# Two-layer decoder trunk on one core: when the MLP's turned hidden features are rounded, and five buffers for raw weight chunks instead of four

## The chip, the cores and the metric

One core of one Trainium2 chip runs the whole trunk in one launch. The metric is the device time of one execution in microseconds. The kernel before has a median of 2459.55 us in three runs (2457.21 to 2461.0).

## What is computed

Batch 1, 256 tokens, width 2048, two layers, all in float32. The part that the change concerns is the MLP of each layer, which has 8192 hidden features:

```python
for i in range(DEPTH):                      # DEPTH = 2
    hn = rmsnorm(h, attn_norm_g[i])
    ...                                     # attention, mixer A or B
    hn = rmsnorm(h, mlp_norm_g[i])
    h = h + jnp.square(jax.nn.relu(hn @ mlp_w1[i])) @ mlp_w2[i]
    gate = jax.nn.sigmoid(rmsnorm(h, ple_norm_g[i]) @ ple_w_gate[i])
    h = h + (p[i] @ ple_w_proj[i]) * gate
return rmsnorm(h, final_norm_g)
```

## The kernel before

**Split products.** Every float32 product is made of three products of rounded numbers. A weight chunk is a tile of 128 x 1024 (512 KB). `load` (L230) brings it from HBM into a `raw` buffer, issued by SP; `copy` (L242) rounds it to `whi` on ScalarE (ACT); `sub` (L250) makes `wlo` = `raw` - `whi` on VectorE (DVE). TensorE (PE) then multiplies `whi` with the high and the low part of the other operand, and `wlo` with the high part. There are 4 buffers `raw`, 6 `whi` and 5 `wlo`.

**The order of the work.** `Program.run` writes one static order. For each chunk, in the order in which PE uses them, it first issues loads as far ahead as the `raw` buffers go (a load waits until the buffer's last reader is done), then the rounding and the subtraction of the chunk some four and three places ahead, then lets every running generator go one `yield` further, then issues PE's matmuls of the chunk. So one `yield` is one chunk of PE's work, and an engine takes its instructions strictly in the order in which they were written: an ACT instruction that waits for a transfer holds up every later `whi`.

**The MLP** (`mlp`). The hidden features are cut into 4 blocks b of 2048, a block into 4 groups q of 512. An "up" gives 256 tokens x 512 features (tokens on partitions); a "down" needs the features on partitions. Groups 0 and 1 of block 0 are made by `ups`, all others two at a time by `up_mixed`, which takes 22 chunk steps: ten of 12 matmuls and three times four steps a, b, t, u of 6, 3, 6 and 6, for which DVE also adds weights (L530 makes `ts`, L535 and L536 change `raw` in place). `downs_pair` follows: 16 chunk steps of 12 matmuls. The order is: ups(0; 0, 1), up_mixed(0; 2, 3), then for each block b: downs_pair(b; 0, 1), up_mixed(b+1; 0, 1), downs_pair(b; 2, 3), up_mixed(b+1; 2, 3). The first downs_pair of a block uses group 2 from its ninth step on and group 3 from its thirteenth.

**How a group is turned** (`up`, called by `up_plain` and by `done` in `up_mixed`; `turned` and `bounce` below it). ACT scales and clips (L798) and squares (L755); DVE transposes 32 x 32 squares into the tile `z` (L699); POOL writes `z` to HBM (`dU`, L196) and, when that has landed, reads it back in another arrangement with four transfers (L200) into `w`, `t` or `y`; ACT rounds the result into the high part of `h` (L763), DVE subtracts for the low part (L765), and PE's downs read `h`. How many `yield`s stand between these steps decides where each is in its engine's order. Before, there are two between square and transpose (for the second group of a mixed pair four: `late` = 2), and one between the end of `turned` and the rounding.

**Elsewhere.** `sum_halves`, `to_head`, `key_unit`, `q_done` and `proj_done` use two small tiles of pool `E`: `es` (written by ACT at L389, read by DVE at L391) and `rsh` (written and read by DVE).

Of the kernel before, what the change touches and what calls it, by code (L numbers as in the profile page):

```python
# [10 lines left out]
F32 = mybir.dt.float32  # L11
# [4 lines left out]
P = 128  # L16
D = 2048
T = 256
# [15 lines left out]
UNIT_AHEAD = (0, 1, 2, 4, 5)  # L34
DMA_AHEAD = 7
SPLIT_AHEAD = 3
RAW_BUFS, HI_BUFS, LO_BUFS = 4, 6, 5
MIXED = (2, 3, 5)

G_ATTN, G_MLP, G_PLE, G_KV, G_FIN = 0, 2, 4, 6, 7  # L40
# [2 lines left out]
def f32(ap):  # L43
    return ap.bitcast(F32)
# [116 lines left out]
def kernel(ctx: ExitStack, tc: tile.TileContext, a: dict, out: bass.AP):  # L161
# [13 lines left out]
    cur = {}  # L175
# [6 lines left out]
    def close_pool(key):  # L182
        cur.pop(key)
        cur.pop(key + "/es").close()
# [200 lines left out]
                nc.tensor.matmul(ps[:, :T], lo[:, col:col + P], rhs[:, :T], start=False, stop=last)  # L385

    def sum_halves(ps):
        s = cur["E"].tile([P, T], F32, tag="es", name="es", bufs=4)
        nc.scalar.copy(s, ps[:, :T])  # L389
        t = cur["E"].tile([P, T], F32, tag="et", name="et", bufs=7)  # L390
        nc.vector.tensor_add(t, ps[:, T:], s)  # L391
        return t
# [203 lines left out]
    def to_head(ps, norm, dst, roped, mark, late=0, lo=None):  # L596

        t = sum_halves(ps)
        for _ in range(1 + late):
            yield  # L600
        while norm.r is None:
            yield
        if callable(dst):
            dst = dst()
        elif dst is None:
            dst = t
        if not roped:
            nc.vector.tensor_mul(dst, t, norm.rb)
        else:
            sh = cur["E"].tile([32, T], F32, tag="rsh", name="rsh", bufs=2)  # L610
            nc.vector.stream_shuffle(sh, t[:32, :], ROPE_SWAP)
            nc.vector.tensor_mul(dst, t, norm.rc)
            nc.vector.tensor_mul(sh, sh, norm.rs)
            nc.vector.tensor_add(dst[:32, :], dst[:32, :], sh)
        if lo is not None:
            yield
            nc.scalar.copy(lo[0], dst)
            yield
            nc.vector.tensor_sub(lo[1], dst, f32(lo[0]))
        mark()  # L620
# [107 lines left out]
    def mlp(layer, xg, norm, to, norm2, opening):  # L728

        y = [None] * 4
        hid = [[None] * 16 for _ in range(NFB)]
        forms = [None] * (KT // 2)

        def new(n):
            return cur["h"].tile([P, D // 2], F32, tag=n, name=n, bufs=1)  # L740

        def row():
            return cur["z"].tile([P, 2, 512], F32, tag="t", name="t", bufs=2)

        def second(n):

            return flat(row()) if n == "z" and hid[-1][-1] else flat(row_tile())

        def other(n):

            return flat(row()) if n == "w" else new(n)

        def up(b, q, t, late=0):

            nc.scalar.activation(t, t, AF.Square)  # L755
            for _ in range(2 + late):
                yield
            w = yield from turned(t, second if b == 0 and q == 1 else other if q % 2 else new, nc.gpsimd)
            yield
            w4 = w.rearrange("p a (i j r) -> p a (i j) r", j=2, r=32)  # L760
            h = cur["z"].tile([P, 2, 4, T], F32R, tag="h", name="h", bufs=4)
            h5 = h.rearrange("p c i (j a r) -> p c a (i j) r", j=2, r=32)
            nc.scalar.copy(h5[:, 0], w4)  # L763
            yield
            nc.vector.tensor_sub(h5[:, 1], w4, f32(h5[:, 0]))  # L765
            for i in range(4):
                hid[b][4 * q + i] = (h[:, 0, i], h[:, 1, i])

        def up_plain(b, q, ps0, ps1, mm):

            while norm.col is None:
                yield
            t = row()
            for j, ps in enumerate((ps0, ps1)):
                nc.scalar.activation(t[:, j], ps, AF.Relu, scale=norm.col[:, j:j + 1])
            yield from up(b, q, t)

        def up_mixed(b, q):

            ts = []  # L780

            def sums(aux):
                s, o = row(), row()
                nc.scalar.copy(s[:, 0], aux["P1"])
                yield
                nc.vector.tensor_sub(s[:, 1], aux["R6"], s[:, 0])
                nc.vector.tensor_add(o[:, 0], aux["Q5"], s[:, 1])
                nc.vector.tensor_sub(s[:, 1], aux["Q7"], s[:, 1])
                nc.vector.tensor_sub(o[:, 1], o[:, 0], aux["Q7"])
                ts.extend((s, o))  # L790

            def done(i, ps):
                while not ts:
                    yield
                t = ts[i]
                nc.vector.tensor_add(t, ps, t)
                for j in range(2):
                    nc.scalar.activation(t[:, j], t[:, j], AF.Relu, scale=norm.col[:, j:j + 1])  # L798
                yield from up(b, q + i, t, 2 * i)

            c0, c1, c2, c3, c4 = [c for c in range(KT // 2) if c not in MIXED]
            m0, m1, m2 = [(c,) for c in MIXED]
            order = [(0, c0), (0, c1), m0, (0, c2), (1, c0), m1, (0, c3), (1, c1), m2, (0, c4), (1, c2), (1, c3), (1, c4)]
            pair_major(lambda i, c: a["w1"][layer * 128 + (b * 4 + q + i) * 8 + c], order, xg, forms, sums, done)

        def normed(k):
            return renorm(k, G_PLE + layer, to, norm2)

        def down(b, q, ps0, ps1, mm):
            if b == 0:  # L810
                y[q] = row_tile()
            for j, ps in enumerate((ps0, ps1)):
                if b:
                    nc.vector.tensor_add(y[q][:, j], ps, y[q][:, j])
                else:
                    nc.scalar.copy(y[q][:, j], ps)
            if b < NFB - 1:
                return
            yield
            w = yield from turned(y[q], second if q == 1 else new)  # L820
            add_turned(q, w)
            yield
            yield from in_pairs(normed, q)

        def chunks(w, b, q):
            return lambda c: a[w][layer * 128 + (b * 4 + q) * 8 + c]

        def ups(b, q, hooks=None):
            token_major(chunks("w1", b, q), xg, lambda *ps: up_plain(b, q, *ps), hooks, whole=True)

        def downs(b, q):
            token_major(chunks("w2", b, q), hid[b], lambda *ps: down(b, q, *ps), whole=True)

        def all_forms():
            for c in MIXED:
                yield from x_forms(2 * c, G_MLP + layer, forms)
                yield
        taken_late(lambda: ups(0, 0, {4: [lambda: norm.factor(rows=True)]}), lambda: ups(0, 1), opening,
                   [all_forms])
        def downs_pair(b, q):  # L840
            taken_late(lambda: downs(b, q), lambda: downs(b, q + 1))

        up_mixed(0, 2)
        for b in range(NFB):
            downs_pair(b, 0)
            if b < NFB - 1:
                up_mixed(b + 1, 0)
                downs_pair(b, 2)
                up_mixed(b + 1, 2)
        downs(NFB - 1, 2)  # L850
        downs(NFB - 1, 3)
        prog.op(lambda: close_pool("z"))
        prog.op(lambda: open_pool("j"))

    def flat(t):
        return t.rearrange("p j c -> p (j c)")

    def row_tile():

        return cur["h"].tile([P, 2, 512], F32, tag="y", name="y", bufs=4)  # L860
# [14 lines left out]
    def ple(layer, pg, xg, norm, nxt, norm2, last):  # L875
# [182 lines left out]

        for q in range(4):
            def proj_done(f, ps, q=q):  # L1060
                s = cur["E"].tile([P, T], F32, tag="es", name="es", bufs=4)
                nc.scalar.copy(s, ps[:, :T])
                t = cur["j"].tile([P, T], F32, tag="pj", name="pj", bufs=8)
                nc.vector.tensor_add(t, ps[:, T:], s)
                pj[4 * q + f] = t
                return
                yield
# [321 lines left out]
    def key_unit(n, i, which, at, hooks=None):  # L1389

        def done(ps0, ps1, mm):
# [3 lines left out]
            for g in range(GB):  # L1395
# [2 lines left out]
                k4, c4, s4 = (v.rearrange("p (j a r) -> p j a r", j=2, a=4) for v in  # L1398
                              (cur["E"].tile([P, T], F32, tag="et", name="et", bufs=7), n_b1.rc, n_b1.rs))
                src = w.rearrange("p a (g j r) -> p g j a r", j=2, r=32)[:, g]  # L1400
                sh = cur["E"].tile([32, T], F32, tag="rsh", name="rsh", bufs=2)
                sh4 = sh.rearrange("p (j a r) -> p j a r", j=2, a=4)
                nc.vector.tensor_mul(k4, src, c4)
                nc.vector.stream_shuffle(sh4, src[:32], ROPE_SWAP)
# [215 lines left out]

    def q_done(h, ps):
        t = sum_halves(ps)
        sh = cur["E"].tile([32, T], F32, tag="rsh", name="rsh", bufs=2)
        nc.vector.stream_shuffle(sh, t[:32, :], ROPE_SWAP)
        nc.vector.tensor_mul(t, t, n_b1.rc)
        nc.vector.tensor_mul(sh, sh, n_b1.rs)
        nc.vector.tensor_add(t[:32, :], t[:32, :], sh)
        yield
        d = q_tile()
        nc.scalar.copy(d[:, :T], t)  # L1630
        nc.vector.tensor_sub(d[:, T:], t, f32(d[:, :T]))
        qT[h] = d
# [239 lines left out]
```

## Time and profile before

| | before |
|---|---|
| median of 3 runs | 2459.55 us |
| the profiled execution | 2455.63 us |
| its span, first to last instruction | 2453.9 us |
| PE busy | 2430.5 us |
| DVE busy | 1829.8 us |
| ACT busy | 1385.2 us |
| mean granted TensorE clock | 0.999 |

The profiled execution lies 3.9 us below the median; 1.7 us of its time are outside the span. A matmul's end is modelled in the profile: a 128x512 matmul is given 0.39 us, while the next one starts 0.23 us after it. So a gap between two matmuls is shown about 0.16 us shorter than PE really lost.

### The profile page before, as it was taken

How to read it: one execution, taken by the hardware profiler on the slowest of the kernel's cores; microseconds unless marked ns; L12 is line 12 of the kernel's file. 1: busy time of each engine (PE TensorE's matmuls, PEld its weight loads, DVE VectorE, ACT ScalarE, POOL GpSimd, SP SyncE). 2: the span in 40 equal slices, each digit the busy share in tenths (PEclk: the TensorE clock that was granted, in tenths of full speed). 3: DMA queues.
4: the chain of work that ended last, by engine and by line, in shares of the span. 5: the costliest groups of instructions: out<-in, count | busy, mean ns of one | idle time of the engine just before them, and what ended most of it. 6: DMA issues, size and time to landing. Idle time of an engine off the chain costs nothing.

```text
span 2453.9 us, 33107 instructions
## 1 busy us (share of the span) xinstructions
PE 2430.5 (99%) x11721; PEld 2041.4 (83%) x11721; DVE 1829.8 (75%) x2716; ACT 1385.2 (56%) x2001; POOL 97.2 (4%) x182
## 2 busy tenths in 40 slices
PE   9999999999999999999999999999999999999998
PEld 8888888887888888887888889988788888888887
DVE  7866687786777787676778989867676677668766
ACT  6544444565555554554564788756555555455556
POOL 0000000000000000000000000000000000000000
PEclk9999999999999999999999999999999999999999
DMA  7666666767666766678776743476766676676875
GB/s 276 200 218 211 198 207 196 231 202 233 224 209 222 240 209 218 225 234 256 245 240 210 259 159 121 139 234 219 228 205 218 230 235 203 223 232 213 264 231 162
DMA packets 162662, 532.27 MB, mean 217 GB/s; under 512 B 19584, under 2 KB 35392, under 8 KB 162496
## 3 DMA queue, kind: packets, MB, share of 16 engines
q1 hardware_dynamic: 150672, 494.73, 62.1%
q0 software_dynamic: 11248, 34.63, 4.9%
q8 instruction: 92, 1.51, 0.2%
q10 hardware_dynamic: 576, 0.79, 0.1%
q14 instruction: 74, 0.61, 0.1%
HBM read 496.00 MB, written 34.08 MB: 216 GB/s over the span
## 4 chain that ended last, share of the span: by engine, by line
PE 81%; issue 7%; DMA 7%; DVE 2%; ACT 2%; POOL 1%; SPq 0%; ACTq 0%; DVEq 0%; POOLq 0%
PE at L588 20%; PE mm L588 20%; PE at L492 14%; PE mm L383 11%; PE mm L385 6%; PE mm L492 3%; DMA t<-dU 2%; DMA w<-dU 2%; ACT whi L242 1%; PE at L383 1%; DMA dU<-z 1%; DVE wlo L250 1%; DMA raw<-in_w 1%; DMA dU<-y 1%; PE at L385 1%
## 5 line engine op out<-in xcount | busy, mean ns | idle before, releaser
L250 DVE TENSOR_TENSOR wlo<-raw,whi 128x1024 fp32r<-128x1024 f32 (+1 forms) x917 | 1081.1, 1191 | 367.4 <-ACT whi L242 140.8
L242 ACT CAST whi<-raw 128x1024 fp32r<-128x1024 f32 (+1 forms) x917 | 929.9, 1029 | 584.0 <-DMA raw<-in_w 144.2
L492 PE MATMUL at<-whi,xa 128*128 128x512 f32 x1288 | 396.6, 389 | 0.0
L383 PE MATMUL mm<-xa,whi 128*128 128x512 f32 x1104 | 371.7, 395 | 0.0
L588 PE MATMUL mm<-whi,h 128*128 128x512 f32 x1024 | 318.4, 391 | 10.3 <-ACT h L763 5.3
L588 PE MATMUL at<-whi,h 128*128 128x512 f32 x1024 | 315.1, 389 | 0.0
L492 PEld LDWEIGHTS at<-whi,xa 128*128 128x128 f32 x1288 | 241.7, 188 | 50.3 <-ACT whi L242 0.4
L385 PE MATMUL mm<-xa,wlo 128*128 128x256 f32 x1104 | 273.2, 278 | 0.0
L492 PE MATMUL at<-wlo,xa 128*128 128x512 f32 x644 | 250.8, 389 | 1.2 <-DVE wlo L250 1.2
L588 PEld LDWEIGHTS mm<-whi,h 128*128 128x128 f32 x1024 | 192.2, 188 | 55.5 <-DVE h L765 8.2
L588 PEld LDWEIGHTS at<-whi,h 128*128 128x128 f32 x1024 | 192.2, 188 | 39.8
L385 PEld LDWEIGHTS mm<-xa,wlo 128*128 128x128 f32 x1104 | 207.3, 188 | 18.0
L383 PEld LDWEIGHTS mm<-xa,whi 128*128 128x128 f32 x1104 | 193.3, 188 | 30.5 <-issue 0.4
L588 PE MATMUL at<-whi,xa 128*128 128x512 f32 x672 | 207.4, 390 | 1.5 <-DVE et L391 1.3
L588 PE MATMUL mm<-whi,xa 128*128 128x512 f32 x656 | 202.7, 390 | 0.0
L588 PE MATMUL mm<-wlo,h 128*128 128x512 f32 x512 | 199.3, 389 | 0.0
L588 PE MATMUL at<-wlo,h 128*128 128x512 f32 x512 | 199.2, 389 | 0.0
L588 PEld LDWEIGHTS at<-whi,xa 128*128 128x128 f32 x672 | 124.6, 188 | 26.9 <-issue 1.4
L492 PEld LDWEIGHTS at<-wlo,xa 128*128 128x128 f32 x644 | 120.9, 188 | 27.2 <-DVE wlo L250 2.0
L588 PEld LDWEIGHTS mm<-whi,xa 128*128 128x128 f32 x656 | 122.5, 188 | 25.0
L588 PE MATMUL at<-wlo,xa 128*128 128x512 f32 x336 | 130.9, 390 | 0.5 <-DVE wlo L250 0.5
L588 PE MATMUL mm<-wlo,xa 128*128 128x512 f32 x328 | 127.7, 389 | 0.0
(412 smaller groups left out, 2957.1 us busy)
## 6 DMA issues: line engine op xcount, KB each, us to landing
raw<-in_w SPq DMA_DIRECT2D x512, 512.0 KB, 4.5
raw<-in_w_qk SPq DMA_DIRECT2D x96, 512.0 KB, 3.6
raw<-in_w_gate SPq DMA_DIRECT2D x64, 512.0 KB, 4.4
raw<-in_w_kv SPq DMA_DIRECT2D x48, 512.0 KB, 4.4
raw<-in_w_v SPq DMA_DIRECT2D x47, 512.0 KB, 4.3
raw<-in_w_q SPq DMA_DIRECT2D x32, 512.0 KB, 4.4
raw<-in_w_oB SPq DMA_DIRECT2D x32, 512.0 KB, 3.6
dU<-z POOLq DMA_DIRECT2D x30, 512.0 KB, 6.5
```

What stands on the lines that cost most here:

```text
L242: nc.scalar.copy(hi[:, c], t[:, c])
L250: nc.vector.tensor_sub(lo[:, c], t[:, c], f32(hi)[:, c])
L383: nc.tensor.matmul(ps, hi[:, col:col + P], rhs, start=first, stop=False)
L385: nc.tensor.matmul(ps[:, :T], lo[:, col:col + P], rhs[:, :T], start=False, stop=last)
L492: nc.tensor.matmul(ps, x_, w_, start=b not in touched, stop=end and last[b] == n and i == 2)
L588: nc.tensor.matmul(st[j], *parts[j][i], start=k == i == 0, stop=k == kt - 1 and i == 2)
```

## The change

The rounding of a turned group is written later behind the read-back: four `yield`s instead of one for groups 0 and 1, two instead of one for groups 2 and 3. The second group of a mixed pair is transposed, written and read back one `yield` earlier (`late` = 1 instead of 2). Weights get a fifth `raw` buffer (4 KB in each partition). The pool `E` gives up one `es` buffer of four and one `rsh` buffer of two.

```diff
-RAW_BUFS, HI_BUFS, LO_BUFS = 4, 6, 5
+RAW_BUFS, HI_BUFS, LO_BUFS = 5, 6, 5
...
     def sum_halves(ps):
-        s = cur["E"].tile([P, T], F32, tag="es", name="es", bufs=4)
+        s = cur["E"].tile([P, T], F32, tag="es", name="es", bufs=3)
         nc.scalar.copy(s, ps[:, :T])
...
-            sh = cur["E"].tile([32, T], F32, tag="rsh", name="rsh", bufs=2)
+            sh = cur["E"].tile([32, T], F32, tag="rsh", name="rsh", bufs=1)
             nc.vector.stream_shuffle(sh, t[:32, :], ROPE_SWAP)
...
         def up(b, q, t, late=0):
+            rest = 4 if q < 2 else 2
 
             nc.scalar.activation(t, t, AF.Square)
             for _ in range(2 + late):
                 yield
             w = yield from turned(t, second if b == 0 and q == 1 else other if q % 2 else new, nc.gpsimd)
-            yield
+            for _ in range(rest):
+                yield
             w4 = w.rearrange("p a (i j r) -> p a (i j) r", j=2, r=32)
...
-                yield from up(b, q + i, t, 2 * i)
+                yield from up(b, q + i, t, i)
```

The `es` and `rsh` lines change alike at their other places (`proj_done`, `key_unit`, `q_done`). PE's and POOL's instructions are the same in the same order; the lines behind `up` are numbered one or two higher in the changed kernel.

**First place: ACT in up_mixed(0; 2, 3) of layer 0**, the rounding of groups 0 and 1 of block 0 (`h<-w`, `h<-y`). `whi<-raw 128x1024` is one weight chunk, `128x512` the half chunk of a step b, `whi<-ts` a step t. Before:

```order
L242 CAST whi<-ts 128x1024
L763 CAST h<-w 128x4x8x32
L242 CAST whi<-raw 128x1024 x2
L763 CAST h<-y 128x4x8x32
L242 CAST whi<-raw 128x1024 x2
L242 CAST whi<-raw 128x512
L242 CAST whi<-ts 128x1024
```

and in the changed kernel:

```order
L242 CAST whi<-ts 128x1024
L242 CAST whi<-raw 128x1024 x3
L765 CAST h<-w 128x4x8x32
L242 CAST whi<-raw 128x1024
L242 CAST whi<-raw 128x512
L765 CAST h<-y 128x4x8x32
L242 CAST whi<-ts 128x1024
```

The rounding of group 0 stands three weight chunks later, that of group 1 two, inside the second of the three a, b, t, u groups. DVE's subtractions (L765, then L767) move in the same way.

**Second place: DVE behind the same up_mixed**, where groups 2 and 3 of block 0 are turned during downs_pair(0; 0, 1). `t<-at,t` is the last addition of a group, `z<-t` its transpose, `h<-w` and `h<-t` the low parts of groups 2 and 3. Before:

```order
L796 TENSOR_TENSOR t<-at,t 128x1024
L250 TENSOR_TENSOR wlo<-raw,whi 128x1024 x4
L699 STREAM_TRANSPOSE z<-t 128x2x4x4x32
L250 TENSOR_TENSOR wlo<-raw,whi 128x1024 x2
L765 TENSOR_TENSOR h<-w,h 128x4x8x32
L250 TENSOR_TENSOR wlo<-raw,whi 128x1024 x5
L765 TENSOR_TENSOR h<-t,h 128x4x8x32
```

and in the changed kernel:

```order
L798 TENSOR_TENSOR t<-at,t 128x1024
L250 TENSOR_TENSOR wlo<-raw,whi 128x1024 x3
L699 STREAM_TRANSPOSE z<-t 128x2x4x4x32
L250 TENSOR_TENSOR wlo<-raw,whi 128x1024 x4
L767 TENSOR_TENSOR h<-w,h 128x4x8x32
L250 TENSOR_TENSOR wlo<-raw,whi 128x1024 x4
L767 TENSOR_TENSOR h<-t,h 128x4x8x32
```

Group 3's transpose stands one weight chunk earlier, group 2's low part one later, group 3's low part where it stood (eleven chunks behind the addition in both).

**Third place: SP at the start of the kernel**, where the fifth buffer shows first. `raw<-in_w_v` and `raw<-in_w_qk` are weight loads, the others tables. Before:

```order
L230 DMA raw<-in_w_v 128x1024
L1114 DMA gains<-in_gains 128x128
L1115 DMA ident<-in_ident 128x128
L1116 DMA ropeC<-in_ropeCA 32x256
L1117 DMA ropeS<-in_ropeSA 32x256
L1118 DMA mA<-in_mA 128x1024
L230 DMA raw<-in_w_qk 128x1024 x12
```

and in the changed kernel:

```order
L230 DMA raw<-in_w_v 128x1024
L230 DMA raw<-in_w_qk 128x1024
L1116 DMA gains<-in_gains 128x128
L1117 DMA ident<-in_ident 128x128
L1118 DMA ropeC<-in_ropeCA 32x256
L1119 DMA ropeS<-in_ropeSA 32x256
L1120 DMA mA<-in_mA 128x1024
L230 DMA raw<-in_w_qk 128x1024 x11
```

From here on every weight load stands one place earlier against everything else on SP.

More of the change, by code (lines that the diff above doesn't have):

```diff
@@ L1060, in proj_done @@
             def proj_done(f, ps, q=q):
-                s = cur["E"].tile([P, T], F32, tag="es", name="es", bufs=4)
+                s = cur["E"].tile([P, T], F32, tag="es", name="es", bufs=3)
                 nc.scalar.copy(s, ps[:, :T])
@@ L1400, in done @@
                 src = w.rearrange("p a (g j r) -> p g j a r", j=2, r=32)[:, g]
-                sh = cur["E"].tile([32, T], F32, tag="rsh", name="rsh", bufs=2)
+                sh = cur["E"].tile([32, T], F32, tag="rsh", name="rsh", bufs=1)
                 sh4 = sh.rearrange("p (j a r) -> p j a r", j=2, a=4)
@@ L1622, in q_done @@
         t = sum_halves(ps)
-        sh = cur["E"].tile([32, T], F32, tag="rsh", name="rsh", bufs=2)
+        sh = cur["E"].tile([32, T], F32, tag="rsh", name="rsh", bufs=1)
         nc.vector.stream_shuffle(sh, t[:32, :], ROPE_SWAP)
```

## The prediction

> **What bounds the kernel now.** I read the page's first lines, then the list of what PE waited for over the whole span.
>
> ```profile
> span 2453.9 us, 33107 instructions
> PE 2430.5 (99%) x11721; PEld 2041.4 (83%) x11721; DVE 1829.8 (75%) x2716; ACT 1385.2 (56%) x2001; POOL 97.2 (4%) x182
> ...
> PE mm L588 <- ACT h L763: 5.3, 5, 1.7
> PE mm L588 <- DVE h L765: 5.0, 7, 0.8
> ...
> PE at L492 <- DVE wlo L250: 1.2, 2, 0.7
> ...
> PE mm L492 <- DVE wlo L250: 0.6, 2, 0.3
> ```
>
> PE is the bound, and its instructions do not change; the change can only win or lose where PE stands still. In the MLP it stands still for two things: the `h` parts of a turned group in the downs (10.3 us, 12 times) and a late `wlo` in a mixed up (1.8 us, 4 times). What such a stop really costs shows PE's timeline, first where the downs of block 0 begin, then at their ninth step:
>
> ```profile
> 561.61 0.39 PE L492 MATMUL at<-wlo,xa 128*128 128x512 f32 x1
> 561.84 0.62 PE L588 MATMUL mm<-whi,h 128*128 128x512 f32 x2
> ...
> 585.48 0.50 PE L588 MATMUL mm<-whi,h 128*128 128x512 f32 x1 [1.72 <-ACT h L763]
> 586.74 0.50 PE L588 MATMUL mm<-whi,h 128*128 128x512 f32 x1 [0.76 <-DVE h L765]
> 587.07 0.39 PE L588 MATMUL mm<-wlo,h 128*128 128x512 f32 x1
> ```
>
> An undisturbed matmul starts 0.227 us after the last one (twelve, a chunk, take 2.72 us), though it is shown as 0.39 long, so each listed wait hides 0.16 us; and the matmul behind a stop starts 0.33 instead of 0.23 us later, another 0.1. With 0.27 us for each stop, `h` costs 10.3 + 12 x 0.27 = 13.5 us, and with stops too short to be listed I take 14; `wlo` costs 1.8 + 4 x 0.27 = 2.9 us. **The change has at most 17 us, 0.7%, to win in the MLP.** How much of the 14 us falls on block 0 say the same lists for 520 to 606 us (layer 0) and 1696 to 1785 us (layer 1):
>
> ```profile
> PE mm L588 <- ACT h L763: 2.0, 2, 1.7
> PE mm L588 <- DVE h L765: 1.5, 2, 0.8
> ...
> PE mm L588 <- ACT h L763: 2.5, 2, 1.4
> PE mm L588 <- DVE h L765: 1.5, 2, 0.8
> ```
>
> That is 7.5 us in eight stops, with 0.27 each 9.7 us; 4.3 us are left for the six later blocks of the two layers.
>
> **Term 1, the opening (groups 0 and 1 of block 0).** ACT's, DVE's and PE's timelines in up_mixed(0; 2, 3) of layer 0:
>
> ```profile
> 539.70 1.05 ACT L763 CAST h<-y 128x1024 fp32r<-128x1024 f32 x1 [3.72 <-DMA y<-dU]
> ...
> 540.78 1.23 DVE L765 TENSOR_TENSOR h<-y,h 128x1024 fp32r<-128x1024 f32 x1 [2.35 <-ACT h L763]
> 541.92 2.35 DVE L250 TENSOR_TENSOR wlo<-raw,whi 128x1024 fp32r<-128x1024 f32 x2
> ...
> 547.26 1.22 DVE L250 TENSOR_TENSOR wlo<-ts,whi 128x1024 fp32r<-128x1024 f32 x1
> ...
> 543.20 0.50 PE L492 MATMUL at<-wlo,xa 128*128 128x512 f32 x1 [0.46 <-DVE wlo L250]
> ...
> 548.53 0.50 PE L492 MATMUL mm<-wlo,xf 128*128 128x512 f32 x1 [0.28 <-DVE wlo L250]
> ```
>
> ACT stands 3.72 us before the rounding of `h<-y`, whose data PE needs only 30 us later; DVE loses 2.35 us behind it; the first of the two `wlo` of 541.92 ends just before PE's 543.20, the `wlo<-ts` of 547.26 just before 548.53. In the changed order the late chunk's `wlo` stands ahead of both `h`, and ACT gets to `h<-y` after one more whole and one half chunk and `h<-w`, when 539.70 has come. DVE's 2.35 us of idling go, and the two stops are at most 0.62 and 0.44 us long, so both vanish. Against it: the two `h` subtractions (1.23 us each) now stand between the steps of an a, b, t, u group. They only take the place of idle time: the `wlo<-ts` still ends some 1 to 2 us earlier than now. Layer 1 has the same pattern: 2.9 us in all, and PE's downs begin about 1.3 us earlier in layer 0. If the cover fails, the cost stays what it is.
>
> **Term 2, the chain to groups 2 and 3 of block 0.** The chain of waits, followed back from 600 us, shows what sets PE's stops at the ninth and thirteenth step:
>
> ```profile
> 550.93 4.67 DMA raw<-in_w
> ...
> 560.57 1.23 DVE t L796
> ...
> 561.88 1.35 ACT t L798 x2
> ...
> 576.17 8.10 DMA w<-dU
> ...
> 589.27 7.52 DMA t<-dU
> ...
> 597.98 1.24 DVE h L765
> ```
>
> It begins with a raw weight load. The last chunks of the mixed up wait for their `raw` buffer; only then follow `whi`, `wlo`, DVE's sums, ACT's `t`, and the square at 561.88 + 1.35 = 563.2, which is 1.4 us *behind* PE's start on the downs (561.84). From the square to the end of group 3's low part go 599.2 - 563.2 = 36.0 us, while PE wants it twelve chunks and two matmuls after its start: 12 x 2.72 + 0.45 = 33.1 us. So PE loses 1.4 + 36.0 - 33.1 = 4.3 us; the stops of that block make 4.5. **The loss of a block is (square minus PE's start) + 36 - 33.1**, and it is zero from a lead of some 3 us on.
>
> What the fifth buffer does to the lead. The rows on the loads are ACT's wait for them, SP's wait for the buffers, and the transfer itself:
>
> ```profile
> ACT whi L242 <- DMA raw<-in_w: 144.2, 117, 3.8
> ...
> SPq L230 <- DVE wlo L250: 1516.8, 733, 9.7
> ...
> raw<-in_w SPq DMA_DIRECT2D x512, 512.0 KB, 4.5
> ```
>
> A load waits for the subtraction four chunks back, lands 4.5 us after it, and rounding (1.0) and subtraction (1.2) follow: with issue some 7 to 9 us for four chunks, hardly below PE's 2.72 us a chunk. So behind any hold-up ACT and DVE catch up slowly, 117 times waiting for a load. With five, the same load hangs on the subtraction one chunk earlier, 1.2 us earlier where DVE runs without a break. In block 0 the load of 550.93 also profits from DVE being 1 to 2 us ahead (term 1): I take the square 2.5 to 4 us earlier, so at 560.0, with PE's start at 560.5. Loss after: -0.5 + 36.0 - 33.1 = 2.4 us, and about the same in layer 1: 4.9 of 9.7 us remain. **Gain 4.8 us**, bounds 0 (the square moves only with PE) and 9.7 (a lead of 3 us as in the later blocks).
>
> **Term 3, the later blocks**, by block 3 of layer 0:
>
> ```profile
> 1067.25 1.05 ACT L242 CAST whi<-raw 128x1024 fp32r<-128x1024 f32 x1 [1.50 <-DMA raw<-in_w]
> ...
> 1074.81 1.06 ACT L755 ACTIVATE t<-t 128x1024 f32<-128x1024 f32 x1
> ...
> 1096.05 1.05 ACT L763 CAST h<-w 128x1024 fp32r<-128x1024 f32 x1 [4.52 <-DMA w<-dU]
> ...
> 1077.55 0.61 PE L588 MATMUL mm<-whi,h 128*128 128x512 f32 x2
> ...
> 1112.30 0.50 PE L588 MATMUL mm<-whi,h 128*128 128x512 f32 x1 [0.76 <-DVE h L765]
> ```
>
> The lead is 2.7 us and the low part comes 1112.3 - 1074.8 = 37.5 us after the square: loss 37.5 - 2.7 - 33.1 = 1.7 us, the largest of the six. Ahead of the square ACT waits 1.5 us for a load, which five buffers should cover: then 0.2 us are left there, and nothing in the blocks that lose less. **Gain 4 of 4.3 us**, bounds 0 and 4.3.
>
> **The later rounding itself** (`rest` = 2) costs group 2 nothing. Before its `h<-w` ACT idles 4.52 us; now one more `whi` stands ahead, 1.05 us, and even with the longest wait for a load (3.8) that is 4.85, while `h` has another 0.9 us until PE's ninth step (1096.05 + 1.05 + 1.23 = 1098.3 against 1077.55 + 8 x 2.72 = 1099.3). Groups 0 and 1 have over 25 us to spare.
>
> **Group 3 a chunk earlier** (`late` = 1). POOL's timeline:
>
> ```profile
> 567.96 0.56 POOL L196 DMA_DIRECT2D dU<-z  x1 [31.88 <-DVE z L699]
> 574.54 2.18 POOL L200 DMA_DIRECT2D w<-dU  x4 [6.02 <-ACT whi L242]
> 578.28 0.56 POOL L196 DMA_DIRECT2D dU<-z  x1 [1.55 <-DVE z L699]
> 587.64 2.19 POOL L200 DMA_DIRECT2D t<-dU  x4 [8.80 <-issue]
> ```
>
> Group 2's write is read back 6.6 us after its issue, group 3's 9.4 us after, 3.4 us after group 2's reads have landed (576.17 + 8.10 = 584.3). Group 3's write seems to stand behind group 2's reads, so issuing it sooner gives nothing; the transpose moves past one `wlo` (1.2 us), which bounds it: 0 to 1.2 us in each of the blocks that still lose. I take 0. "DMA: Bandwidth & Descriptors" of the Trainium skill, section "Queues, rings and completion order", says that each DMA engine takes the descriptors of one queue in the order of its ring; by that rule this part is worth 0, without it up to 2.4 us more in the two blocks 0, and the 9.4 us agree with the rule. The transpose overwrites `z`, so it waits for group 2's write, which has landed by 574.5; it starts 1.5 us before the write of 578.28, and 1.2 us earlier is still behind it.
>
> **The small tiles.** One row, from ACT's waits:
>
> ```profile
> ACT es L389 <- DVE et L391: 4.1, 4, 2.0
> ```
>
> A third `es` can hold up the fourth of four copies by about these 2 us of ACT, a few times, outside the MLP; PE waits there for nothing that ACT delivers within 2 us. Zero, bounds 0 to 2 us. `rsh` is written and read on DVE alone, in order: zero. The other SP transfers stand behind one more load at the start only: zero.
>
> **Sum**: 2.9 + 4.8 + 4 = 11.7, about 12 us. Against the profiled execution 2455.63 - 12 = 2443.6; the median lies 3.9 us above that execution, so I forecast 2459.55 - 12 = 2447.5 us.
>
> **The rivals.** (1) *All of it*: the fifth buffer gives block 0 the lead of the other blocks; then 17 us go: 2442.5. For it: nothing but the backlog distinguishes block 0. Against: term 2's chain has a load behind the in-place additions that five buffers move only by a subtraction. (2) *The opening alone*: ACT's lead is set by PE giving `whi` buffers back, not by loads; the square keeps its distance to PE and only 2.9 us go: 2456.5. Against it stand the waits of 1.5 us just ahead of the squares. (3) *Slower*: the one more chunk ahead of group 2's rounding is late. Loads and POOL's transfers share the engines; if the wait of that `whi` for its load exceeds 4.52 + 0.9 - 1.05 = 4.4 us (longest now 3.8), PE stops at the ninth step in all eight blocks; at 6 us that is 8 x 1.6 - 2.9 = +10 us: 2469.5. "Issuing engines are not separate DMA queues" on the same page says that transfers from all engines interleave on the same 16 DMA engines, which speaks for it; no run here shows five loads. (4) *Nothing*: the waits close up elsewhere: 2459.5.
>
> **How the numbers follow.** Forecast 0.60 (own range 2444 to 2452), all of it 0.17, the opening alone 0.14, slower 0.05, nothing 0.04. The range reaches from all of it, with 1.5 us for scatter, to the opening alone: 2441 to 2457. A measurement of this kernel tells about 0.2%, 4.9 us, from no change: faster 0.60 + 0.17 and a little of the opening case, 0.78; within 0.17; slower 0.05.
>
> **What would show it.** Term 1 is right if no `wlo` stop of L492 is left near 543 and 1720 us, term 2 if the square of block 0 comes before PE's first `h` matmul and the `h` stops of 520 to 606 us halve, term 3 if no `h` stop is left in the later blocks and ACT's 144 us of waiting for loads fall well below 100. Wrong would be: group 2's `h` becoming the later one, group 3's read-back starting less than 9 us after its write, or new stops of PE in the attention stages.

## The result and the profile after

The changed kernel takes 2444.11 us (median of 4, 2441.67 to 2445.87) against 2458.38 us of the kernel before (median of 4, the three of the forecast's base among them): 14.3 us less, a ratio of 0.9943 with the interval 0.9924 to 0.9963. Against the forecast's own base, 2459.55 us, it is 15.4 us; the forecast was 2447.5 us. Measured a second time beside the experiments, the ratio was 0.9941 (0.9928 to 0.9953). The profiled execution took 2441.67 us, 13.96 us less than the one of before.

First the page's first lines, then PE's waits over the whole span (engine, line, what it waited for: us in total, times, longest):

```profile
span 2439.8 us, 33123 instructions
...
PE 2426.7 (99%) x11721; PEld 2042.3 (84%) x11721; DVE 1832.9 (75%) x2716; ACT 1384.8 (57%) x2001; POOL 97.0 (4%) x182
```

```profile
PE mm L492 <- DVE wlo L250: 1.1, 2, 0.6
...
PE mm L588 <- DVE h L767: 0.8, 1, 0.8
PE mm L588 <- ACT h L765: 0.6, 1, 0.6
```

Of the four rows shown of before, 12.1 us in 16 stops, 2.5 us in 4 stops are left: 1.1 + 0.8 + 0.6. With the 0.27 us that a stop costs beyond its listed wait, 9.6 + 12 x 0.27 = 12.8 us went; that is most of the 14.0. The two `h` stops left are both in block 0 of layer 0; the later blocks have none. ACT's waits show how little it still stands before weight loads (first row), and that the read-back of `y` is still waited for:

```profile
ACT whi L242 <- DMA raw<-in_w: 28.1, 26, 2.7
...
ACT h L765 <- DMA y<-dU: 7.7, 2, 3.9
```

ACT's waits for these weight loads fell from 144.2 us to 28.1. The chain of waits of the changed kernel, followed back from 597 us, no longer begins with a weight load (columns: start, us, what):

```profile
555.95 5.45 PE at L492 x24
...
565.94 1.15 DVE t L798
...
567.11 1.35 ACT t L800 x2
...
573.41 7.27 DMA w<-dU
...
584.75 8.87 DMA t<-dU
```

It now begins with PE's own matmuls: by the chain they release the `whi` of 561.40, and behind it DVE's last addition and ACT's scaling and square of group 3. The two read-backs of POOL behind it are as slow as they were (7.3 and 8.9 us against 8.1 and 7.5).

**Where the time came from.** The next table compares the start of the same matmul in two traces, that of before and that of each kernel of this study; a negative number is time won in the stretch. Stretches: "opening" is the start of a layer's MLP up to the downs of its block 0, "block 0" from there to the end of the first downs_pair, in which groups 2 and 3 are used, "later" the other blocks.

| us against the trace of before | opening L0 | block 0 L0 | later L0 | opening L1 | block 0 L1 | later L1 |
|---|---|---|---|---|---|---|
| the change | -0.4 | -2.8 | -3.0 | -1.0 | -5.2 | -1.6 |
| the change, second trace | -0.1 | -2.0 | -3.0 | -1.8 | -3.0 | -1.7 |
| five buffers alone | +1.3 | -3.9 | -2.8 | +0.3 | -4.6 | -1.7 |
| new order alone, four buffers | -0.6 | +0.7 | -1.9 | -1.3 | -1.1 | -1.0 |
| small tiles alone | +0.1 | +0.8 | 0.0 | +0.1 | +0.4 | +2.1 |
| change, group 3 as late as before | -0.2 | -2.7 | -3.0 | 0.0 | -1.0 | -1.7 |
| change, rounding as early as before | +1.3 | -4.7 | -3.0 | +0.8 | -5.0 | -1.7 |
| change, group 1 of block 0 still later | -1.4 | -4.7 | -2.8 | -1.8 | -4.7 | -1.7 |

The row of the small tiles, whose schedule in the MLP is that of before, and the two traces of the change show the scatter: up to about 2 us in one cell. Three rows also hold falls of PE's clock (last section), by estimate 1.7 us each: block 0 of both layers of the new order alone and of the small tiles, block 0 of layer 1 with group 3 as late as before. One trace is also one execution: that of before lies 2.7 us under its median, that of the five buffers alone 6.4 us. So the medians say how much, the table only where.

### The profile page after: what moved, and what is told of

Same layout as the page of the kernel before. It is cut to its first block, busy times and chain, and to the rows that moved or that the text cites. A ratio compares the mean times of both kernels' runs of the same rounds, so it can differ in the third digit from the quotient of the medians.

```text
span 2439.8 us, 33123 instructions
## 1 busy us (share of the span) xinstructions
PE 2426.7 (99%) x11721; PEld 2042.3 (84%) x11721; DVE 1832.9 (75%) x2716; ACT 1384.8 (57%) x2001; POOL 97.0 (4%) x182
## 4 chain that ended last, share of the span: by engine, by line
PE 96%; DMA 2%; DVE 1%; ACT 1%; issue 0%; POOL 0%; SPq 0%; ACTq 0%; DVEq 0%
PE at L588 25%; PE mm L588 24%; PE at L492 18%; PE mm L383 11%; PE mm L385 6%; PE mm L492 4%; PE at L383 1%; PE at L385 1%; PE at L1699 1%; DMA t<-dU 0%; PE mm L1723 0%; PE mm L1463 0%; DVE wlo L250 0%; DMA dU<-y 0%; PE mm L932 0%
## 5 line engine op out<-in xcount | busy, mean ns | idle before, releaser
L492 PE MATMUL at<-whi,xa 128*128 128x512 f32 x1288 | 396.6, 389 | 0.0
L492 PEld LDWEIGHTS at<-whi,xa 128*128 128x128 f32 x1288 | 241.8, 188 | 50.3
L492 PE MATMUL at<-wlo,xa 128*128 128x512 f32 x644 | 250.5, 389 | 0.0
L492 PEld LDWEIGHTS at<-wlo,xa 128*128 128x128 f32 x644 | 120.9, 188 | 25.1
```

What stands on the lines that cost most here:

```text
L492: nc.tensor.matmul(ps, x_, w_, start=b not in touched, stop=end and last[b] == n and i == 2)
```

## The experiments

Each kernel was timed beside the kernel before on its chip; a ratio is always to that. "The change" below means the changed kernel.

**Five buffers alone**: the kernel before with the buffers and the small tiles of the change, and the old order.

```diff
-RAW_BUFS, HI_BUFS, LO_BUFS = 4, 6, 5
+RAW_BUFS, HI_BUFS, LO_BUFS = 5, 6, 5
...
-        s = cur["E"].tile([P, T], F32, tag="es", name="es", bufs=4)
+        s = cur["E"].tile([P, T], F32, tag="es", name="es", bufs=3)
```

> The kernel before with the fifth raw buffer and the smaller es and rsh, and none of the later rounding. My theory (the terms add): the fifth buffer alone brings the squares of groups 2 and 3 forward, so the h stops of PE shrink by 8 to 13 us, while both wlo stops of each opening stay (ACT still stands before the early rounding of groups 0 and 1): 8 to 13 us faster than before, ACT's 144 us of waiting for raw<-in_w fall below 60. Rival A (the later rounding does it, buffers are idle): within 2 us of before. Rival B (each is worth little without the other): 3 to 6 us faster. On the read-back of group 1 in the opening, which landed at 539.7 before and at 543.3 after: if five loads in flight slow it, it lands near 543 here too.

Measured: 2450.72 us, ratio 0.9953 (0.9939 to 0.9967). In its trace, the fastest of six executions, ACT's waits for `raw<-in_w` fall to 11.8 us and the `h` stops to 0.6 us; but new stops stand in the opening (PE's and ACT's timelines there):

```profile
543.06 0.73 PE L492 MATMUL at<-whi,xa 128*128 128x512 f32 x2 [0.74 <-ACT whi L242]
...
549.85 0.50 PE L492 MATMUL mm<-wlo,xf 128*128 128x512 f32 x1 [0.27 <-DVE wlo L250]
```

```profile
541.02 1.05 ACT L763 CAST h<-y 128x1024 fp32r<-128x1024 f32 x1 [4.99 <-DMA y<-dU]
...
562.18 1.06 ACT L755 ACTIVATE t<-t 128x1024 f32<-128x1024 f32 x1
```

With five buffers and the old order ACT stands 4.99 us before `h<-y`, 1.3 us longer than before: it gets there when it did, at 536.0, and the data come later (541.02 instead of 539.70). Even so the square comes before PE's first `h` matmul (563.18): a lead of 1.0 us instead of -1.4. In this trace the buffer alone does the work of terms 2 and 3; by the medians it wins 9.5 us, as expected.

**The new order alone**: the change with four `raw` buffers and the old small tiles.

```diff
-RAW_BUFS, HI_BUFS, LO_BUFS = 5, 6, 5
+RAW_BUFS, HI_BUFS, LO_BUFS = 4, 6, 5
...
```

> The changed kernel with four raw buffers again (es and rsh as before): only the later rounding and the earlier transpose. My theory: one or both wlo stops of each opening go, and with ACT less behind, a part of the stops in block 0; the stops of the later blocks stay: 2 to 5 us faster than before, ACT's wait for raw<-in_w stays above 100 us. Rival A (the later rounding does it): 10 to 14 us faster. Rival B (each is worth little without the other): within 2 us of before. If five loads in flight had slowed the read-back of group 1, it lands near 540 here, as before; if it is the place of the transfers in the program that matters, near 543.

Measured: 2451.16 us, ratio 0.9958 (0.9946 to 0.9971), more than the 2 to 5 us that I expected. ACT waits 195.6 us for loads, more than before, and one of these waits hits group 2's rounding (ACT's timeline, block 0 of layer 0, then PE's):

```profile
578.35 1.05 ACT L242 CAST whi<-raw 128x1024 fp32r<-128x1024 f32 x1 [2.18 <-DMA raw<-in_w]
583.70 1.04 ACT L242 CAST whi<-raw 128x1024 fp32r<-128x1024 f32 x1 [4.30 <-DMA raw<-in_w]
584.65 1.04 ACT L765 CAST h<-w 128x1024 fp32r<-128x1024 f32 x1
```

```profile
585.74 0.51 PE L588 MATMUL mm<-whi,h 128*128 128x512 f32 x1 [2.37 <-ACT h L765]
587.19 0.79 PE L588 MATMUL mm<-whi,h 128*128 128x512 f32 x1 [0.95 <-DVE h L767]
587.78 0.63 PE L588 MATMUL mm<-wlo,h 128*128 128x512 f32 x1
588.21 1.05 PE L588 MATMUL mm<-whi,h 128*128 128x512 f32 x2
```

`h<-w` has no wait of its own: it stands behind the one `whi` more that the new order puts ahead of it, and that waits 4.30 us for its load. This is the mechanism of the rival "slower", with four buffers; the stop is 2.37 us where before had 1.72. The two halves of the change win some 9 to 12 us each (9.5 and 9.1 by the medians, 11.6 and 10.3 by the ratios) and together 14: they are not additive, since each removes some of the same stops, and the fifth buffer keeps the new order from making one of its own. How much the new order adds once the fifth buffer is there is not shown: the interval of the ratio of five buffers alone, 0.9939 to 0.9967, overlaps those of the change.

**The small tiles alone**: the kernel before with three `es` and one `rsh`.

```diff
-        s = cur["E"].tile([P, T], F32, tag="es", name="es", bufs=4)
+        s = cur["E"].tile([P, T], F32, tag="es", name="es", bufs=3)
...
-            sh = cur["E"].tile([32, T], F32, tag="rsh", name="rsh", bufs=2)
+            sh = cur["E"].tile([32, T], F32, tag="rsh", name="rsh", bufs=1)
```

> The kernel before with three es and one rsh, four raw buffers. My theory: no difference (within 2 us of before), ACT's waits at L389 for L391 stay below 7 us. Rival (a buffer less makes ACT wait for DVE in the attention stages): 2 to 5 us slower, with PE stops there that before does not have.

Measured: 2461.11 us, ratio 1.0002 (0.9991 to 1.0013). The room for the fifth buffer costs nothing.

**Group 3 as late as before**: the change with `late` = 2.

```diff
-                yield from up(b, q + i, t, i)
+                yield from up(b, q + i, t, 2 * i)
```

> The changed kernel with late = 2 again for the second group of a mixed pair: its transpose, write and read-back stand one chunk later. My theory (its write stands behind the reads of the first group anyway): within 2 us of the changed kernel, and the read-back starts at the same distance (3 to 5 us) after the first group's reads have landed. Rival (the earlier issue brings the data earlier): group 3's h comes 1 to 2.7 us later in every block and the stops at the thirteenth step return: 4 to 12 us slower than the changed kernel.

Measured: 2445.16 us, ratio 0.9933 (0.9919 to 0.9946); the change itself has 0.9943 and 0.9941. One chunk earlier is worth nothing that these runs resolve, as expected. POOL's timeline in block 0 of layer 0, of the change and then of this kernel:

```profile
571.78 2.18 POOL L200 DMA_DIRECT2D w<-dU  x4 [6.09 <-ACT whi L242]
574.32 0.56 POOL L196 DMA_DIRECT2D dU<-z  x1 [0.36 <-DVE z L699]
583.12 2.18 POOL L200 DMA_DIRECT2D t<-dU  x4 [8.24 <-ACT whi L242]
```

```profile
572.49 2.18 POOL L200 DMA_DIRECT2D w<-dU  x4 [6.48 <-DMA dU<-z]
575.77 0.56 POOL L196 DMA_DIRECT2D dU<-z  x1 [1.10 <-DVE z L699]
585.03 2.18 POOL L200 DMA_DIRECT2D t<-dU  x4 [8.71 <-ACT whi L242]
```

From the reads of group 2 to those of group 3 it is 11.3 us in the change and 12.5 us here; the write is issued 0.7 us sooner after those reads, and the reads follow it after 8.8 and 9.3 us. The `whi` that the brackets name is not what the reads waited for: the write of 574.32 lands 8.3 us after its issue, and the reads are issued 0.54 to 0.57 us behind the landing in all eight blocks. Over all eight blocks the reads of group 3 start on average 23.4 us after group 2's square in the change, 24.4 us here, and 9.4 and 9.3 us after their write. The reads do move when the write is issued sooner; what that wins is not seen in the time.

**Group 3's transfers on SP's queue.**

```diff
-            w = yield from turned(t, ..., nc.gpsimd)
+            w = yield from turned(t, ..., nc.sync if q == 3 else nc.gpsimd)
```

> The changed kernel with group 3's write and read-back issued by SP, between the weight loads, instead of by POOL behind group 2's. My theory of the record (on POOL's queue the write stands behind group 2's reads): its read-back starts 5 to 7 us after the write instead of 9.4, and h of group 3 comes 2 us or more earlier. Rival (the 16 engines are busy with weight loads, whichever queue issues): still 8 to 10 us after the write. For the time I expect within 3 us of the changed kernel either way, since little is left to win there; SP waiting for the write to land can hold up weight loads and cost up to 5 us.

Measured: 2443.19 us, ratio 0.9928 (0.9912 to 0.9943): as the change. SP's timeline in block 0 of layer 0, and SP's waits:

```profile
574.59 0.61 SPq L196 DMA_DIRECT2D dU<-z  x1
575.70 1.46 SPq L230 DMA_DIRECT2D raw<-in_w  x2
583.19 1.75 SPq L200 DMA_DIRECT2D t<-dU  x4
```

```profile
SPq L200 <- DMA dU<-z: 47.0, 16, 7.0
```

On another queue, with no read of group 2 ahead of it, the read-back still starts 8.6 us after its write, not after the 5 to 7 that I expected; over the eight blocks it is 8.3 us on average, against 9.4 and 8.9 in the two traces of the change. The write takes as long to land (8.3 us on average, against 8.9 and 8.3), so POOL's queue does not make the distance. What did come sooner are the data: the last of the four reads lands 6.1 us after the first is issued, instead of 10.5, `h<-t` starts 30.4 us after group 2's square instead of 33.3, and in none of the eight blocks does PE stop for group 3. But SP, which issues the weight loads, stands 47.0 us, ACT's waits for loads rise from 28.1 to 49.4 us, and little was left to win. Whether the queue or the loads held up meanwhile make these reads faster, this run does not separate.

**The rounding as early as before**: the change with one `yield` between read-back and rounding for every group.

```diff
-            rest = 4 if q < 2 else 2
+            rest = 1
```

> The changed kernel with rest = 1 everywhere: five raw buffers and the earlier transpose, but the rounding of every group as early as before. Against raw5_alone it shows the earlier transpose by itself, against the changed kernel the later rounding by itself. My theory (the later rounding is worth only the opening once there are five buffers, the earlier transpose about 1 us of the read-back of group 3): the two wlo stops of each opening are there as in raw5_alone (2 to 3 us more than in the changed kernel), h stops of the later blocks gone; 2444 to 2449, that is 0 to 4 us slower than the changed kernel. Rival (the later rounding also keeps ACT ahead in every block): h stops return in the later blocks, 5 to 10 us slower than the changed kernel.

Measured: 2446.23 us, ratio 0.9941 (0.9925 to 0.9957): no difference to the change, as expected. Its stops are those of the five buffers alone in the opening, and none at `h`:

```profile
PE at L492 <- ACT whi L242: 1.5, 2, 0.8
PE at L492 <- DVE wlo L250: 1.4, 2, 0.7
```

The later rounding wins some 1.7 us in each opening and does not end up ahead: opening and block 0 together, both layers, are 7.6 us won here, 9.4 and 6.9 us in the two traces of the change. What is won in the opening brings PE sooner to the wait for groups 2 and 3. (Outside the table this trace loses 2.5 us against that of before: a stop at 1350 us is 2.17 us long, 1.27 before, and the clock falls behind it.)

**Group 1 of block 0 still later**: its rounding moves behind the last a, b, t, u group.

```diff
-            rest = 4 if q < 2 else 2
+            rest = (7 if b == 0 and q else 4) if q < 2 else 2
```

> The changed kernel with rest = 7 instead of 4 for group 1 of block 0 alone, so that its rounding stands behind the last a, b, t, u group of the mixed up instead of inside the second one. My theory (in the changed kernel the read-back of group 1 landed at 543.3 instead of 539.7, so ACT stood 3.9 us before it in the middle of the group and the wlo<-ts came late): the stops at 548 and 1719 go, the squares of block 0 come 1 to 2 us earlier and its h stops shrink: 1.5 to 4 us faster than the changed kernel. Rival (DVE's own additions make wlo<-ts late): the two stops stay within 0.3 us of what they are, no gain.

Measured: 2438.46 us, ratio 0.9911 (0.9896 to 0.9926). ACT's timeline, for which the change's own stands in the next section, then PE's waits:

```profile
541.98 1.05 ACT L242 CAST whi<-ts 128x1024 fp32r<-128x1024 f32 x1 [2.73 <-PE at L492]
...
545.82 1.05 ACT L765 CAST h<-y 128x1024 fp32r<-128x1024 f32 x1
...
558.28 1.06 ACT L756 ACTIVATE t<-t 128x1024 f32<-128x1024 f32 x1
```

```profile
PE at L588 <- DVE wlo L250: 0.4, 1, 0.4
PE mm L588 <- DVE h L767: 0.2, 1, 0.2
```

ACT no longer waits for `y`, the `wlo` are in time, the square is 2.1 us earlier than in the change, and with PE's downs at 560.38 its lead is 2.1 us: no `h` stop in block 0 of layer 0. The gain is more than the 1.5 to 4 us over the change that I expected. Here the opening's gain is kept; I read that so: what held PE in the opening (ACT before `h<-y`) held the square too.

**The same with group 3 on SP's queue.**

> Both of the last two edits together. My theory: no PE stop above 0.5 us is left in the MLP but for chance, 2 to 5 us faster than the changed kernel. Rival (SP's wait costs loads): slower than group1_later by 1 to 5 us.

Measured: 2440.72 us, ratio 0.9919 (0.9903 to 0.9934), 2.3 us above the one without it, as the rival said. SP's queue brings no time here either.

**The change and the kernel with group 1 still later, the best of these, once more, side by side.**

> The changed kernel itself, on the same chip and in the same rounds as the next run. My theory: 2442 to 2447, the read-back of group 1 in the opening of layer 0 lands between 543 and 544, one wlo stop of 0.5 to 1 us is left in each opening, and what is left of the h stops of block 0 differs from the first profile by chance (0 to 3 us in a layer).

> group1_later once more, beside the changed kernel. My theory: 3 to 7 us faster than the changed kernel, and no wlo stop in the openings. Rival (the 5.6 us between their medians came from different chips and rounds): within 2 us of the changed kernel.

Measured: 2446.07 us for the change, 2438.41 us for the best kernel, ratio 0.9912 (0.9898 to 0.9925): 7.7 us below the change on the same chip, a little more than the 3 to 7 that I expected, and it beats both kernels. Of the two `wlo` stops that I expected of the change, one in each opening, its second trace has the one of layer 0 alone. By the traces the openings and block 0 together win 12.6 us in the best kernel, 9.4 and 6.9 us in the change.

## Why the prediction was right, and where its sizes were off

**The sum.** In the traces of before and of the change the three terms come to 1.4 + 8.0 + 4.6 = 14.0 us, the whole difference of the two profiled executions; the forecast had 11.7. That the sum came closer than its terms is luck: term 1 was 1.5 us too large, term 2 3.2 us too small. Another 1.5 us of the forecast's miss lie in a term that I had held fixed: the median of the change lies 2.4 us above its profiled execution, not 3.9.

**Term 1, the opening: forecast 2.9 us, measured 1.4 (1.9 in the second trace).** The step that failed is "ACT gets to `h<-y` after one more whole and one half chunk and `h<-w`, when 539.70 has come". The order was as told, the time of the data was not. ACT's, DVE's and PE's timelines of the change:

```profile
543.30 1.05 ACT L765 CAST h<-y 128x1024 fp32r<-128x1024 f32 x1 [3.94 <-DMA y<-dU]
```

```profile
544.39 1.23 DVE L767 TENSOR_TENSOR h<-y,h 128x1024 fp32r<-128x1024 f32 x1 [1.81 <-ACT h L765]
...
546.86 1.22 DVE L250 TENSOR_TENSOR wlo<-ts,whi 128x1024 fp32r<-128x1024 f32 x1
```

```profile
548.13 0.50 PE L492 MATMUL mm<-wlo,xf 128*128 128x512 f32 x1 [0.62 <-DVE wlo L250]
```

The first stop (543.20 before) is gone. At the second place the data of `y` come at 543.30 instead of 539.70, ACT stands 3.94 us where it stood 3.72, now inside an a, b, t, u group, and DVE stands behind it again: `wlo<-ts` ends at 548.08, and PE stops for 0.62 us. The data come 3.6 us later for two reasons. The write of `y` lands later, so its four reads are issued from 535.01 us on instead of 533.89; and from the issue of the last read to its landing it is 6.5 us instead of 4.0. Transfers issued between 526 and 545 us (KB each, median us to landing), before and after, then the reads of `y` in the five buffers alone and in the new order alone:

```profile
raw<-in_w SPq DMA_DIRECT2D x6, 512.0 KB, 4.0
...
y<-dU POOLq DMA_DIRECT2D x4, 128.0 KB, 3.9
```

```profile
raw<-in_w SPq DMA_DIRECT2D x6, 512.0 KB, 7.1
...
y<-dU POOLq DMA_DIRECT2D x4, 128.0 KB, 5.6
```

```profile
y<-dU POOLq DMA_DIRECT2D x4, 128.0 KB, 3.5
...
y<-dU POOLq DMA_DIRECT2D x4, 128.0 KB, 4.5
```

The windows of 535 to 543 us (columns: us; busy time of PE, PEld, DVE, ACT and POOL; granted clock; busy share of the DMA engines; GB/s), before and after:

```profile
535.00:543.00 8.00, 7.74 (x35) 6.07 (x33) 5.65 (x6) 4.28 (x6) 1.07 (x2) 1.00 0.78 239
```

```profile
535.00:543.00 8.00, 8.00 (x37) 6.63 (x36) 7.54 (x8) 4.36 (x6) 2.18 (x4) 1.00 0.93 269
```

The share went from 0.78 to 0.93, and the reads took 5.6 us instead of 3.9. In the five buffers alone `y` came at 541.02, in the kernel with the early rounding at 540.89, in four traces with the new order and five buffers at 543.3 to 543.7. So five buffers alone do not slow the reads; they are issued 1.3 us later there (535.16), and that is all. The new order alone slows them by less (the last one lands 5.4 us after its issue, at 541.6), both together most. I read it so: with the rounding moved, ACT goes on to the next chunks, buffers come free, and three weight loads are issued beside the reads (536.32 to 538.59; three in the new order alone too) where before and the five buffers alone issue two (from 537.3 on). A run that holds these loads back is missing. I had taken a landing time from the trace of before as given, and it is one that the change moves. The rule of the Trainium skill that was cited for the rival "slower" ("DMA: Bandwidth & Descriptors", section "Issuing engines are not separate DMA queues") agrees with these rows; it bore on term 1 as well, and I weighed it only for that rival. So the sign that I had named, no `wlo` stop of L492 left near 543 and 1720 us, came half: two of four are left. And no median shows this term: with five buffers, rounding early or late gives the same one.

**Term 2, block 0: forecast 4.8 us, measured 8.0 (5.0 in the second trace).** The mechanism was right, the sizes were small. The formula (chain from the square to group 3's low part, less the lead, less 33.1 us) holds within 0.4 us in each of these traces (where no subtraction is quoted, it is taken as 1.23 us behind ACT's 1.05):

| layer 0 | square | PE's downs | lead | chain | loss by the formula | stops of groups 2 and 3, with 0.27 each |
|---|---|---|---|---|---|---|
| before | 563.2 | 561.84 | -1.4 | 36.0 | 4.3 | 4.6 |
| the change | 560.42 | 561.45 | 1.0 | 35.6 | 1.5 | 1.9 |
| the change, second trace | 560.68 | 561.57 | 0.9 | 36.4 | 2.4 | 2.7 |
| five buffers alone | 562.18 | 563.18 | 1.0 | 34.5 | 0.4 | 0.5 |
| early rounding | 562.08 | 563.01 | 0.9 | 32.9 | none | none |
| group 1 still later | 558.28 | 560.38 | 2.1 | 33.9 | none | none |

It fails for the new order alone: lead -1.1 and chain 34.1 give 2.2 us, the stops make 3.9, all at the ninth step. There group 2's `h` had become the later one, which I had named as a sign of being wrong; the one short stop of the five buffers alone, 0.26 us, is at the ninth step too. The rows of the change in this table, ACT's and then PE's timelines:

```profile
560.42 1.06 ACT L756 ACTIVATE t<-t 128x1024 f32<-128x1024 f32 x1
...
593.72 1.05 ACT L765 CAST h<-t 128x1024 fp32r<-128x1024 f32 x1 [6.32 <-DMA t<-dU]
```

```profile
561.45 0.62 PE L588 MATMUL mm<-whi,h 128*128 128x512 f32 x2
...
594.82 0.49 PE L588 MATMUL mm<-whi,h 128*128 128x512 f32 x1 [0.57 <-ACT h L765]
596.08 0.50 PE L588 MATMUL mm<-whi,h 128*128 128x512 f32 x1 [0.76 <-DVE h L767]
```

The lead came out at 1.0 us where I took 0.5, and the square at 560.42 where I took 560.0. What was mis-sized is the constant 36.0: the chain took 32.9 to 36.4 us in the five rows with five buffers, and in layer 1 of the change 32.9, so nothing was left to lose there. The listed `h` stops of 520 to 606 us fell from 3.5 to 1.3 us, more than halved as told (to 1.9 in the second trace). The read-backs make the scatter; why one takes 7 and another 9 us is not settled.

**Term 3, the later blocks: forecast 4 of 4.3 us, measured 4.6 and 4.7** in the two traces (4.5 with five buffers alone): no `h` stop of a later block is left, and ACT's 144.2 us of waiting are 28.1. The fifth buffer wins it alone, as told; but the new order alone, with four buffers, also wins 2.9 us there, which I had not seen.

**The later rounding costs group 2 nothing**: right with five buffers, where PE shows no stop at the ninth step of the change's first trace and 0.26 us in the second. With four, PE's stop there was 2.37 us in block 0 of layer 0 against 1.72 before: the zero rests on the fifth buffer. I had worked it out from block 3, where there was room; in block 0 before, group 2's `h` was already late.

**Group 3 a chunk earlier, 0**: the size was right, the reason was not. I had its write stand behind group 2's reads on POOL's queue. The reads start 1.0 us earlier when the write does, and on SP's queue, with nothing of group 2 ahead, 8.6 us after the write; less than 9 us after it, which I had named as a sign against me, came in the change as well (8.8 in block 0). "Queues, rings and completion order" of the Trainium skill's page "DMA: Bandwidth & Descriptors", which tells the order in a ring of the queues of SP and ACT, is not contradicted by that, but it does not explain the distance. The distance is the time that the write takes to land: group 2's lands after 6.0 us on average, group 3's, with group 2's four reads under way beside it, after 8.9. That those reads and the weight loads slow it fits the rows above; it is argued, not shown by a run that leaves them out.

**The small tiles, 0**: right.

**The rivals.** "The opening alone" fell: the square did move against PE. "All of it" was nearly reached: 14.3 of 17 us; what is missing is half of term 1 and the 1.9 us left in block 0 of layer 0. "Slower" exists as a mechanism, with four buffers. "Nothing" fell with the measured time.

## What to carry to other kernels

An engine that runs in order and meets a wait for a transfer holds up everything behind it; look for the consumer that needs the data last and write the wait just ahead of it, and check that the next engine's wait does not move along: here the same ACT wait held PE's weights and the square of the next groups, so moving it clear of both won 7.7 us more than moving it halfway. A landing time read from the trace is an outcome, not a constant: here a change of buffers and order moved one by 3.6 us. And a gain ahead of a wait that another chain sets is only kept if that chain starts earlier too.

## What the runs showed of the hardware

After some stops PE's clock fell, and the length of the last one does not say after which. In the new order alone PE stood 2.37 us before 585.74, and the window behind it has a granted clock of 0.71 (columns as above):

```profile
585.00:590.00 5.00, 3.31 (x8) 2.41 (x9) 4.59 (x4) 3.83 (x4) 2.18 (x4) 0.71 0.92 306
```

In its timeline above matmuls start 0.43 us apart behind the stop, instead of 0.23: the lower of the clock's two levels, 1.2 instead of 2.4 GHz. Before, the stop of 1.72 us at the same place left the clock of these 5 us at 1.00. So a stop's price had another term there, of some 0.2 us for each matmul at the lower level; from the granted clock of 0.72 between 586 and 592 us I estimate it at 6 x 0.28 = 1.7 us. Such falls stand in four of the twelve traces: behind stops of 2.37 and 1.08 us in the new order alone, 2.63 and 1.55 us with the small tiles alone, 1.34 us with group 3 as late as before and 2.17 us with the early rounding. But 1.74 us, at 1355 us in the new order alone, had none. What decides is not settled here.

This bears on the medians. Of the 37 executions of the kernel before that were timed beside the experiments, six had a mean granted clock of 0.999 (2458.0 us on average), 16 of 0.998 (2459.6), ten of 0.997 (2462.1) and five of 0.996 (2465.0). The change had 0.999 in six of nine and 0.998 in the others, the kernel with group 1 still later 0.999 in all ten. So a kernel with fewer stops also ran more of its time at the full clock; how much of the 14.3 us that makes is not separated. Between the two profiled executions it makes nothing: neither has such a fall, and the 14.0 us came without it.
